# A new list schedule for the first six tiles: two transposes by DMA, weights in smaller pieces, two loads queued earlier

## The chip, the cores and the metric

The kernel runs on one core of one Trainium2 chip. The metric is the device time of one execution in microseconds (us). Each comparison ran both kernels in turn on the same chip. Profiles are of single executions; their span is about 2 us shorter than the execution's time.

## The reference

```python
# x: (8, 1024, 768) float32, w_qkv: (768, 2304) float32, gamma: ones, eps: 1e-5
def reference(x, gamma, w_qkv, eps):
    rms = np.sqrt(np.mean(x ** 2, axis=-1, keepdims=True) + eps)
    x_norm = x / rms * gamma
    return np.matmul(x_norm, w_qkv).astype(np.float32)
```

The 8,192 rows make 64 tiles of 128 rows. K = 768 is six blocks of 128. The result of a tile is 2,304 columns: four products' worth of 512 and one of 256, each summed over the six blocks in PSUM, the buffer that TensorE's results go to.

## The kernel before

TensorE (PE in the profiles) does the products; VectorE (DVE), ScalarE (ACT) and GpSimd (POOL) scale weights and share the casting and copying; SyncE (SP) issues the DMA transfers. A tile needs x transposed (K on the partitions). Tiles 6 to 63 get that by a transposing DMA; tiles 0 to 3, and before the change 4 and 5, by TensorE. The first six tiles, the "head", are computed while the weights arrive, so their order is a hand-made list with planned times. The list only sorts the instructions; at run time each engine takes its own in that order and waits on semaphores. All loads of x and of weights, all stores and all DMA transposes go through SyncE's one queue.

```python
ARRIVALS = "xxxwwwxwwwwwxxwww"     # order of the head's loads: x tiles, weight pieces
PIECES = [... six of (one K block, columns 0:512), (0, 3, 512, 512), (3, 6, 512, 512),
          (0, 6, 1024, 512), (0, 6, 1536, 512), (0, 6, 2048, 256)]   # k0, k1, column, columns
HEAD_PLAN = [ ... (16.47, "cast", 4, "DVE"), ... (17.24, "tr", 4), ... (18.02, "cp", 4, "DVE"), ...]
...
def tr(t):                         # transpose on TensorE, into PSUM; cp copies it out
    for ko in range(KO):
        nc.tensor.transpose(out=PT[t][:, ko, :], in_=XB[t][:, ko * P:(ko + 1) * P], identity=ident)

def trans_dma(t):                  # transpose by DMA, straight to SBUF
    nc.sync.dma_start_transpose(out=XT[t], in_=XB[t])
...
# a store is put one plan-us after the evacuation that completes its 1,024 columns
elif left[t, h] == 0:
    at(time + gap, store, t, h, *PARTS[h])
...
for t in range(HEAD, MT):          # the steady tiles
    at(now - 15, load_x, t)
    at(now - 8.5, cast, t)
    at(now - 7.5, trans_dma, t)
    at(now - 5, stat, t)
    at(now - 3, recip, t)
    for n0 in range(0, N, NT):
        at(now, mm, t, n0, range(KO))
        ...
```

## Time and profile before

| | before |
|---|---|
| time, median of 3 | 389.47 us (389.18 to 389.60) |
| profiled span | 387.9 us |
| TensorE busy | 379.5 us, 98% |
| steady tile | 5.83 us |
| DMA | 308 GB/s on average, 379 to 397 while the head loads and stores |
| waits of TensorE after 15 us | one, 0.4 us, tile 7's transposed x |

The lines themselves stand in the prediction. In the timeline a row is a run of equal instructions on one engine: start, length, engine, line, operation, output and inputs, count, and in brackets the engine's idle time before it with what ended it. The windows view gives, for a stretch of time, each engine's busy time with its instructions in brackets, then the granted TensorE clock, the DMA engines' busy share and their GB/s.

Bookkeeping helps here: a product of 512 columns starts 0.216 us after the one before. A larger distance between starts is a wait, and these distances give TensorE's lost time a little more truly than the idle times in brackets, since busy times are drawn longer (0.38 us) than the pace.

### The profile page before, as it was taken

To read this page: it belongs to the slowest core of one execution; us is meant where nothing else is said; L and a number is where in the kernel's file an instruction comes from. 1 tells how busy PE (TensorE), PEld (TensorE's weight loads), DVE (VectorE), ACT (ScalarE), POOL (GpSimd) and SP (SyncE) were. 2 spreads that over 40 slices of the span, in tenths; PEclk is the share of its full clock that TensorE was granted. 3 is DMA by queue.
4 is the path that set the end of the run, shared out by engine and by line. 5 is a ranking of instruction groups with operands and counts; after the bars stand their busy time and mean duration, and the time that the engine had idled before them with its cause. 6 is when DMAs were issued, how large, how long until landed. Compare 5 with 4: busy or idle time off the path is not lost.

```text
span 387.9 us, 5500 instructions
## 1 busy us (share of the span) xinstructions
PE 379.5 (98%) x1953; PEld 194.3 (50%) x1992; DVE 159.1 (41%) x317; ACT 178.1 (46%) x359; POOL 5.9 (2%) x12
## 2 busy tenths in 40 slices
PE   7999999999999999999999999999999999999996
PEld 6444644554554554554554554554554554554553
DVE  3667634343433343433343433343334343334332
ACT  6652234544444544444534444534434535434532
POOL 1310000000000000000000000000000000000000
PEclk9999999999999999999999999999999999999999
DMA  7999999999999999999999999999999999999974
GB/s 272 392 384 358 308 369 284 397 301 274 333 311 305 279 326 295 290 330 300 276 346 288 302 317 280 318 311 304 287 318 301 297 318 303 287 325 292 292 264 189
DMA packets 87606, 119.51 MB, mean 308 GB/s; under 512 B 50710, under 2 KB 59676, under 8 KB 87580
## 3 DMA queue, kind: packets, MB, share of 16 engines
q1 hardware_dynamic: 87568, 119.17, 100.7%
q8 instruction: 15, 0.25, 0.3%
q14 instruction: 11, 0.09, 0.1%
q10 hardware_dynamic: 12, 0.00, 0.0%
HBM read 32.25 MB, written 75.50 MB: 278 GB/s over the span
## 4 chain that ended last, share of the span: by engine, by line
PE 94%; DMA 3%; SPq 1%; issue 1%; DVE 0%; ACT 0%
PE pm L216 94%; DMA w_f<-in_w_qkv_dram 2%; DMA xT<-xb 2%; SPq L140 0%; SPq L145 0%; PE pm L183 0%; DVE w_b L151 0%; ACT ot L232 0%; DVE ot L230 0%
## 5 line engine op out<-in xcount | busy, mean ns | idle before, releaser
L216 PE MATMUL pm<-w_b,xT 128*128 128x512 bf16 (+1 forms) x1881 | 372.4, 357 | 3.0 <-DMA xT<-xb 0.4
L216 PEld LDWEIGHTS <-xT 128*128 128x128 bf16 x1920 | 187.6, 98 | 186.6 <-issue 0.8
L230 DVE TENSOR_SCALAR ot<-pm,rstd 128x512 f32<-128x512 f32 (+1 forms) x168 | 116.7, 696 | 210.3 <-PE pm L216 210.3
L232 ACT ACTIVATE ot<-pm,rstd 128x512 f32<-128x512 f32 (+1 forms) x152 | 97.9, 645 | 187.0 <-PE pm L216 141.7
L170 ACT ACTIVATE sq<-x_t 128x768 bf16<-128x768 f32 x64 | 53.4, 834 | 10.2 <-DMA x_t<-in_x_dram 10.2
L159 DVE CAST xb<-x_t 128x768 bf16<-128x768 f32 x61 | 33.2, 545 | 4.1 <-DMA x_t<-in_x_dram 4.0
L172 ACT ACTIVATE rms<-ssq,eps_sb 128x1 f32<-128x1 f32 x64 | 18.8, 294 | 2.1
L170 ACT ACTIVATION_READ_ACCUMULATOR sq<-x_t 128x1 f32 x64 | 12.2, 191 | 0.0
L177 DVE RECIPROCAL rstd<-rms 128x1 f32<-128x1 f32 x64 | 9.8, 153 | 0.0
L151 DVE TENSOR_SCALAR w_b<-w_f,g_sb 128x512 bf16<-128x512 f32 (+1 forms) x14 | 6.5, 494 | 6.1 <-DMA w_f<-in_w_qkv_dram 6.0
L153 ACT ACTIVATE w_b<-w_f,g_sb 128x512 bf16<-128x512 f32 (+1 forms) x10 | 6.1, 651 | 5.7 <-DMA w_f<-in_w_qkv_dram 5.7
L155 POOL TENSOR_SCALAR w_b<-w_f,g_sb 128x512 bf16<-128x512 f32 (+1 forms) x6 | 5.2, 864 | 23.5 <-DMA w_f<-in_w_qkv_dram 23.5
L265 PE MATMUL pm<-warm 128*128 128x128 bf16 x35 | 3.8, 300 | 1.0 <-DVE eps_sb L124 1.0
L265 PEld LDWEIGHTS <-warm 128*128 128x128 bf16 x35 | 3.5, 142 | 1.0 <-DVE eps_sb L124 1.0
L197 PE MATMUL pm<-ident_f,x_t 128*128 128x128 f32 x18 | 2.8, 292 | 0.8 <-DMA x_t<-in_x_dram 0.8
L197 PEld LDWEIGHTS pm<-ident_f,x_t 128*128 128x128 f32 x18 | 2.2, 155 | 1.1 <-DMA x_t<-in_x_dram 1.0
L127 ACT ACT_TABLE_LOAD x1 | 1.3, 1283 | 1.3 <-PEq L325 1.3
L159 DVE CAST xT<-pm 128x512 bf16<-128x512 f32 (+1 forms) x3 | 1.7, 596 | 0.0
L159 DVE COPY xT<-pm 128x768 bf16<-128x768 bf16 x3 | 1.6, 547 | 0.0
L248 DVE COPY g_sb<-pm 128x6 f32<-128x6 f32 x1 | 0.2, 165 | 3.6 <-PE pm L247 3.6
L183 PEld LDWEIGHTS <-xb 128*128 128x128 bf16 x18 | 1.2, 98 | 0.9 <-DVE xb L159 0.6
L183 PE MATMUL pm<-ident,xb 128*128 128x128 bf16 x18 | 1.5, 220 | 0.0
(13 smaller groups left out, 3.1 us busy)
## 6 DMA issues: line engine op xcount, KB each, us to landing
out_dram<-ot SPq DMA_DIRECT2D x126, 512.0 KB, 4.0
x_t<-in_x_dram SPq DMA_DIRECT2D x64, 384.0 KB, 4.3
out_dram<-ot SPq DMA_DIRECT2D x64, 128.0 KB, 3.2
w_f<-in_w_qkv_dram SPq DMA_DIRECT2D x2, 1536.0 KB, 13.3
w_f<-in_w_qkv_dram SPq DMA_DIRECT2D x3, 768.0 KB, 8.5
w_f<-in_w_qkv_dram SPq DMA_DIRECT2D x6, 256.0 KB, 5.8
out_dram<-ot SPq DMA_DIRECT2D x4, 256.0 KB, 2.0
xT<-xb SPq DMA_TRANSPOSE x58, 4.4
```

The source lines that it names most:

```text
L151: nc.vector.tensor_scalar(out=o, in0=i, scalar1=g, scalar2=None, op0=mult)
L153: nc.scalar.activation(out=o, in_=i, func=AF.Copy, scale=g, bias=0.0)
L155: nc.gpsimd.tensor_scalar(out=o, in0=i, scalar1=g, scalar2=1.0, op0=mult, op1=mult)
L159: nc.vector.tensor_copy(out=out, in_=in_)
L170: nc.scalar.activation(out=sq, in_=X[t], func=AF.Square, accum_out=ssq)
L172: nc.scalar.activation(out=rms, in_=ssq, func=AF.Sqrt, scale=inv_k, bias=eps_sb)
L177: nc.vector.reciprocal(out=r, in_=RS[t])
L197: nc.tensor.transpose(out=PT[t, h][:, ko - k0, :], in_=X[t][:, ko * P:(ko + 1) * P], identity=ident_f)
L216: nc.tensor.matmul(out=PM[t, n0][:, :nl], lhsT=XT[t][:, ko, :], rhs=w_b[:, ko, n0:n0 + nl], start=(b == 1), stop=(b == KO))
L230: nc.vector.tensor_scalar(out=o, in0=pm[:, :nl], scalar1=RS[t], scalar2=None, op0=mult)
L232: nc.scalar.activation(out=o, in_=pm[:, :nl], func=AF.Copy, scale=RS[t], bias=0.0)
L265: nc.tensor.matmul(out=wps, lhsT=warm, rhs=warm, start=True, stop=True)
```

## The change

The intent is to take 12 transposes off TensorE, to let weights be scaled as soon as a smaller piece has landed, and to have x of tiles 6 and 7 early. The order of the products in the head changes with it: tiles 0 to 3 do three column blocks before tiles 4 and 5 begin.

```diff
-ARRIVALS = "xxxwwwxwwwwwxxwww"
-PIECES = [..., (0, 3, 512, 512), (3, 6, 512, 512), (0, 6, 1024, 512), (0, 6, 1536, 512), (0, 6, 2048, 256)]
+HEAD = 6
+PIECES = [..., (0, 2, 512, 512), (2, 4, 512, 512), (4, 6, 512, 512), (0, 3, 1024, 512), (3, 6,
+          1024, 512), (0, 3, 1536, 512), (3, 6, 1536, 512), (0, 6, 2048, 256)]
+LOADS = [
+    (-9.00, "x", 0), (-8.99, "x", 1), (-8.98, "x", 2), (-8.97, "w", 0), (-8.96, "w", 1),
     ... cut: pieces 2 to 9, x tiles 3 and 4
+    (-8.85, "w", 10), (-8.84, "x", 5), (18.73, "t", 4), (18.74, "w", 11), (22.11, "t", 5),
+    (22.12, "w", 12), (22.13, "w", 13), (22.14, "x", 6), (22.15, "x", 7),
+]
 HEAD_PLAN = [
     ... the whole list is new; "tr" and "cp" of tiles 4 and 5 are gone
 ]
-HEAD_END = 44.51
+HEAD_END = 43.73
@@ the loads of the head
+    for time, kind, n in LOADS:
+        at(time, {"x": load_x, "w": load_w, "t": trans_dma}[kind], n)
@@ the steady tiles
-        at(now - 15, load_x, t)
+        if ("x", t) not in {q[1:] for q in LOADS}:
+            at(now - 15, load_x, t)
```

## The prediction

> **What bounds the kernel now.** I read the page from the top, then zoomed into the first 60 us, the only part that the change touches (six "head" tiles of 128 rows that are computed while the weights are still arriving; tiles 6 to 63 then run one after the other). The summary and the group of matrix products:
> ```profile
> span 387.9 us, 5500 instructions
> PE 379.5 (98%) x1953; PEld 194.3 (50%) x1992; DVE 159.1 (41%) x317; ACT 178.1 (46%) x359; POOL 5.9 (2%) x12
> ...
> PEclk9999999999999999999999999999999999999999
> DMA  7999999999999999999999999999999999999974
> ...
> L216 PE MATMUL pm<-w_b,xT 128*128 128x512 bf16 (+1 forms) x1881 | 372.4, 357 | 3.0 <-DMA xT<-xb 0.4
> ```
> The reader is to see one bound, TensorE, with 3.0 us idle ahead of its products in the whole run. The chain of waits gives their pace: its repeating pieces of 9.46, 9.46 and 10.10 us, with 0.05 between, hold 150 recorded products plus a missing one here and there, five tiles in 29.16 us: 5.83 us a tile, 0.216 us for a product of 512 columns (24 a tile) and half for one of 256 (6). 64 tiles need 64 x 5.83 = 373.2 us. So the change can win only what stands between the products in the head, and whatever it makes TensorE wait is lost for good.
>
> The timeline of TensorE, start to end:
> ```profile
> 8.48 2.10 PE L216 MATMUL pm<-w_b,xT 128*128 128x512 bf16 x8 [0.39 <-POOL w_b L155]
> 10.52 0.51 PE L183 MATMUL pm<-ident,xb 128*128 128x128 bf16 x6
> 11.19 6.80 PE L216 MATMUL pm<-w_b,xT 128*128 128x512 bf16 x30 [0.15 <-DVE w_b L151]
> 17.82 0.50 PE L183 MATMUL pm<-ident,xb 128*128 128x128 bf16 x6
> 18.20 0.81 PE L216 MATMUL pm<-w_b,xT 128*128 128x512 bf16 x2
> 18.85 0.50 PE L183 MATMUL pm<-ident,xb 128*128 128x128 bf16 x6
> 19.18 31.94 PE L216 MATMUL pm<-w_b,xT 128*128 128x512 bf16 x165
> 51.56 0.60 PE L216 MATMUL pm<-w_b,xT 128*128 128x512 bf16 x2 [0.44 <-DMA xT<-xb]
> ```
> Three groups of six transposes stand between products; from 19.18 on nothing stops TensorE until 51.56, where tile 7 waits for its transposed x. At 19.18, 138 of the head's 180 products are left (102 of 512 columns, 36 of 256): 22.0 + 3.9 = 25.9 us, so tile 6 begins at 45.1.
>
> TensorE is not the only full engine: the DMA row is full too, and the third view, the timeline of the DMA queue (start, time to issue), tells how late its work lands:
> ```profile
> 19.83 7.14 SPq L236 DMA_DIRECT2D out_dram<-ot  x6
> 27.27 0.34 SPq L140 DMA_DIRECT2D x_t<-in_x_dram  x1
> ...
> 38.37 1.95 SPq L206 DMA_TRANSPOSE xT<-xb  x1
> ```
> The first store, issued at 19.83, lands 10.8 us later, at 30.7 (the view of the store's line in that window). The load of tile 6, issued at 27.27, is used at 37.78: VectorE and ScalarE start on it only then, both released by that transfer. One queue, in order, about 10 us deep.
>
> **What the Trainium skill says.** "DMA: Bandwidth & Descriptors", section "Queues, rings and completion order": each DMA engine consumes its descriptors in ring order, and all that SyncE issues shares one row of rings. The trace agrees: late-issued small transfers land only after the big ones ahead. "TensorE: Matmul & The Clock Gate", section "Wait — 56ns, not 53.3ns?": warm products start 55.6 ns (128 columns) and 215.7 ns (512) apart; the trace has 0.216 us, and the chain has 0.34 us for six transposes, 57 ns each. Same page, "What's actually happening": after an idle window of some 3.4 us the clock falls to half, and it takes about as long a busy stretch to come back. The trace shows the fall: the last product ends at about 384.4, and the granted clock is 1.00 in 384.4:386.8 and 0.52 in 386.8:387.9.
>
> **The change part by part.**
> 1. Transposes of tiles 4 and 5 leave TensorE: 12 x 57 ns = 0.68 us saved; their two copies out of PSUM leave VectorE, which has room.
> 2. First weights: piece 0 is now scaled on VectorE (0.49 us against GpSimd's 0.69), piece 1 on GpSimd. All the same the fifth weight piece lands when it did (the bytes ahead of it are the same, 11.3 us), and by its scaling at 11.8 TensorE has done 12 products and 6 transposes in both kernels. So 0 gained.
> 3. Weights of columns 512 to 1535 in halves and thirds, so that scaling starts on smaller pieces: removes the wait of about 0.13 us near 14.5 (two starts 0.345 apart instead of 0.216). TensorE's order becomes tiles 0 to 3 on three column blocks, then tiles 4 and 5. With no wait, from the 24th product on (14.44), tile 4 begins after 48 more, 14.44 + 10.37 = 24.8; tile 5 at 28.7; tile 6 after 15.55 more, at 44.25. That is 0.85 ahead of 45.1, and agrees with the 0.78 by which the schedule's own end moves.
> 4. Loads of tiles 6 and 7 go earlier, so tile 7's wait, about 0.6 us of TensorE time by its start-to-start gap, should go. Best case: 0.85 + 0.6 = 1.45 us faster.
> 5. The two transposes by DMA, and here I see the loss. The built program shows the queue's order: loads, transpose of tile 4, piece 11 (768 KB), four stores of 512 KB, **then** the transpose of tile 5, then pieces 12 and 13, tiles 6 and 7. Ahead of tile 5's transpose stand six x tiles (2,304 KB), 12 weight pieces (5,376 KB) and four stores (2,048 KB): 9,728 KB. In the old kernel its first store was the end of just that many, 9,216 + 512 = 9,728 KB, and landed at 30.7. Add the two transposes' own time on the DMA engines. Those of 38.37 and 45.48 took 6.1 and 6.0 us to land, and around the first of them the DMA moved 79 GB/s in 42:44 against 393 in 8.4:18. From the landings I take 0.6 to 2 us each. Tile 5's xT lands at 31.9 to 34.7, say 33.3.
> 6. Tile 4's transpose is issued after its cast, at about 19.7 to 20.7, and with 6 us to landing is there at 25.7 to 26.7, against a need at 24.8: 1 to 2 us of wait, but it only shifts time: tile 5 would then be wanted at about 29.7 and wait some 3.6.
> The sum: tile 5 begins at 33.3 instead of 28.7, so tile 6 at 33.3 + 15.55 = 48.85, and tile 7 at 54.7 against 51.56: +3.1 us. A wait of over 3 us may also drop the clock for a while: half speed for up to 3.4 us costs up to 1.7 us, at perhaps one chance in three to one half: +0.5. Later waits look safe: pieces 12 and 13 land near 35.5 and 37.5 and are wanted at 41 and 45; tile 6's xT is there before 46.
>
> **The rivals.** (a) The schedule holds as written: 1.45 us faster, 388.0. For it: it was presumably planned with known arrival times. Against it: it scales piece 12 only 3 us after piece 11, which leaves room for one piece (2 us) and a transpose, not for 2 MB of stores (4.9 us at the 1.22 us per 512 KB I read between landings), though the queue has them between. (b) The stores overtake nothing but the transposes stall the DMA queue more, 2 us and over each, and tile 7 or 8 waits again behind the stores of columns 1024 to 2047, which now come in a burst (each tile's 512 KB every 0.65 us instead of every 1.3): 394 to 396. (c) DMA slack swallows it: the DMA engines run slightly ahead or transposes cost little (0.6 us each), so tile 5 waits 2 us only: about 390.5. A bound by VectorE or ScalarE I don't see: 41 and 46% busy.
>
> **Range and chances.** 389.47 + 3.1 + 0.5 - 0.4 (I give (a) and (c) some weight) = 392.7. From 389.6, (c) with a small wait, to 395.2, (b). 2% is 7.8 us: a gain of that is impossible, since the products alone need 373 of a span of 387.9 and the other 15 are start and drain that the change keeps; a loss of that needs several rivals at once. Faster 0.01, same 0.95, slower 0.04.
>
> **What will show it.** In TensorE's timeline: 6 L183-type transposes instead of 18; a wait for xT of 0.5 to 2 us near 25, and a longer one, 2.5 to 4.5 us, ending near 33, with a DMA transpose as releaser and the first store's landing well before it; tile 7 without a wait, or under 0.5. In the DMA queue's timeline the second transpose issued behind four stores, its landing 6 us or more after issue. In the clock row, perhaps a slice under 9 near 33. I am wrong if xT of tile 5 is there by 29 (stores that don't hold it back), or if the stall of the DMA at a transpose is far over 2 us.

## The result

The changed kernel took 397.91 us (median of 4, 397.73 to 398.67) against 389.54 for the kernel before: ratio 1.0219, 95% interval 1.0201 to 1.0237. It is slower by over 2%. (A ratio is the mean time of one kernel's runs over that of the other's in the same rounds, so it is not quite the ratio of the medians quoted. Executions over 1.5% slower than the fastest of the same kernel are left out of the means.) On another chip, later, the same file was 396.57 and 396.38 us with ratios of 1.0163 and 1.0153: under 2% there, and 6.3 to 8.4 us slower in all three comparisons.

From the page of the changed kernel, the summary, the clock row and the group of products:

```profile
span 395.6 us, 5525 instructions
PE 384.1 (97%) x1980; PEld 194.2 (49%) x1980; DVE 156.3 (40%) x312; ACT 177.6 (45%) x357; POOL 8.1 (2%) x17
...
PEclk9996999999999999999999999999999999999999
...
L229 PE MATMUL pm<-w_b,xT 128*128 128x512 bf16 (+1 forms) x1920 | 377.1, 359 | 6.1 <-DMA xT<-xb 5.3
```

Idle time before the products rose from 3.0 to 6.1 us, 5.3 of it for xT. Busy time rose too, by 4.6 us, with 12 transposes fewer, and the clock row has a 6 in its fourth slice. (The group counts 1920 products against 1881 before because the old trace lacks some records; each leaves a hole of 0.05 us in the chain, so 39 of them explain about 2 us of the busy time.) So there are waits, and products that ran slowly. TensorE's timeline of the changed kernel:

```profile
11.78 0.51 PE L196 MATMUL pm<-ident,xb 128*128 128x128 bf16 x6
12.38 16.99 PE L229 MATMUL pm<-w_b,xT 128*128 128x512 bf16 x78
33.77 24.23 PE L229 MATMUL pm<-w_b,xT 128*128 128x512 bf16 x120 [4.40 <-DMA xT<-xb]
58.91 16.41 PE L229 MATMUL pm<-w_b,xT 128*128 128x512 bf16 x81 [0.91 <-DMA xT<-xb]
```

Tile 5 waited 4.4 us, and tile 7, at 58.91, waited longer than it did before. The DMA queue's timeline (start, time to issue) and the chain of waits around it:

```profile
20.29 1.32 SPq L219 DMA_TRANSPOSE xT<-xb  x1
21.67 0.57 SPq L158 DMA_DIRECT2D w_f<-in_w_qkv_dram  x1
22.34 2.71 SPq L249 DMA_DIRECT2D out_dram<-ot  x4
25.14 1.73 SPq L219 DMA_TRANSPOSE xT<-xb  x1
```
```profile
25.14 8.58 DMA xT<-xb
33.72 0.05 issue
```

Tile 5's transpose was issued at 25.14 behind four stores and landed 8.58 us later, at 33.72. The store ahead of it landed at 32.9 in the trace. Now the windows view: DMA around the first transpose, and the clock after the long wait.

```profile
18.00:20.50 2.50, 2.50 (x13) 1.16 (x12) 1.81 (x4) 1.74 (x3) 0.98 (x1) 1.00 1.04 383
20.50:22.50 2.00, 2.00 (x11) 0.88 (x9) 1.53 (x5) 1.36 (x4) 0.00 (x0) 1.00 0.73 174
22.50:25.00 2.50, 2.50 (x13) 1.18 (x12) 1.79 (x5) 2.01 (x5) 0.00 (x0) 1.00 0.66 85
25.00:31.50 6.50, 4.37 (x21) 1.76 (x18) 3.40 (x5) 1.29 (x2) 0.98 (x1) 1.00 1.03 395
...
32.40:39.10 6.70, 5.33 (x13) 1.94 (x14) 0.75 (x1) 0.91 (x2) 2.92 (x5) 0.50 1.06 350
```

The last two columns show the DMA dropping from 383 GB/s to 174 and 85 for 4.5 us; the third from the end shows the clock at half in 32.4:39.1. From 33.77 to 39.1 products start 0.427 us apart, about 12 of them, 12.4 x 0.211 = 2.6 us more than at full clock.

In order of time the loss in this execution, measured between starts of tiles: tile 6 would have begun at 33.77 + 15.55 = 49.3 at full clock, against 45.1 before: 4.2 us. The halved clock adds 2.6. Tile 7 waits 1.07 us against 0.61 before (distance to its start, less the pace): 0.5. A wait of 0.23 at tile 10. Together 7.5 of the 7.7 us by which the span grew. This is an account of where time went, not yet of what causes it: the experiments show that these terms do not add freely.

### The profile page after: what moved, and what is told of

Its sections match the earlier page's. It is cut to its first block, busy times and chain, and to the rows that moved or that the text cites. A ratio compares the mean times of both kernels' runs of the same rounds, so it can differ in the third digit from the quotient of the medians.

```text
span 395.6 us, 5525 instructions
## 1 busy us (share of the span) xinstructions
PE 384.1 (97%) x1980; PEld 194.2 (49%) x1980; DVE 156.3 (40%) x312; ACT 177.6 (45%) x357; POOL 8.1 (2%) x17
## 4 chain that ended last, share of the span: by engine, by line
PE 91%; DMA 7%; SPq 1%; issue 0%; DVE 0%; ACT 0%
PE pm L229 91%; DMA xT<-xb 5%; DMA w_f<-in_w_qkv_dram 2%; SPq L158 0%; SPq L153 0%; DVE w_b L164 0%; ACT ot L245 0%
## 5 line engine op out<-in xcount | busy, mean ns | idle before, releaser
L229 PE MATMUL pm<-w_b,xT 128*128 128x512 bf16 (+1 forms) x1920 | 377.1, 359 | 6.1 <-DMA xT<-xb 5.3
L243 DVE TENSOR_SCALAR ot<-pm,rstd 128x512 f32<-128x512 f32 (+1 forms) x166 | 115.1, 695 | 220.9 <-PE pm L229 220.8
L245 ACT ACTIVATE ot<-pm,rstd 128x512 f32<-128x512 f32 (+1 forms) x154 | 99.5, 647 | 193.0 <-PE pm L229 145.4
L166 ACT ACTIVATE w_b<-w_f,g_sb 128x512 bf16<-128x512 f32 (+1 forms) x6 | 3.8, 648 | 14.1 <-DMA w_f<-in_w_qkv_dram 14.1
L168 POOL TENSOR_SCALAR w_b<-w_f,g_sb 128x512 bf16<-128x512 f32 (+1 forms) x11 | 7.4, 686 | 30.9 <-DMA w_f<-in_w_qkv_dram 23.2
L174 ACT CAST xT<-pm 128x256 bf16<-128x256 f32 (+1 forms) x3 | 1.2, 438 | 1.2 <-PE pm L210 1.2
L172 DVE COPY xT<-pm 128x768 bf16<-128x768 bf16 x1 | 0.6, 558 | 0.0
L196 PEld LDWEIGHTS <-xb 128*128 128x128 bf16 x6 | 0.3, 98 | 0.4 <-DVE xb L172 0.4
```

The source lines that it names most:

```text
L166: nc.scalar.activation(out=o, in_=i, func=AF.Copy, scale=g, bias=0.0)
L168: nc.gpsimd.tensor_scalar(out=o, in0=i, scalar1=g, scalar2=1.0, op0=mult, op1=mult)
L172: nc.vector.tensor_copy(out=out, in_=in_)
L229: nc.tensor.matmul(out=PM[t, n0][:, :nl], lhsT=XT[t][:, ko, :], rhs=w_b[:, ko, n0:n0 + nl], start=(b == 1), stop=(b == KO))
L243: nc.vector.tensor_scalar(out=o, in0=pm[:, :nl], scalar1=RS[t], scalar2=None, op0=mult)
L245: nc.scalar.activation(out=o, in_=pm[:, :nl], func=AF.Copy, scale=RS[t], bias=0.0)
```

## The experiments

Sixteen runs, each a variant of the changed kernel unless said otherwise. The question was first whether tile 5's transpose waits for the stores, then where the rest comes from when that wait is taken away. All results were correct.

### t5_first: the four stores behind tile 5's transpose

```diff
-            at(time + gap, store, t, h, *PARTS[h])
+            at(22.115 if (t, h) in {(1, 0), (2, 0), (3, 0), (0, 0)} else time + gap, store, t, h, *PARTS[h])
```

> Only the queue's order is changed: the four stores of 512 KB go behind the transpose of tile 5 instead of ahead of it. Theory A (in-order queue, the transpose of tile 5 waits for 2 MB of stores): its landing moves from 33.7 us to about 29, TensorE's 4.4 us wait falls below 1.5 us, the clock stays at full, and the time falls by 4.5 to 7 us from 397.9, to 391 to 393.5. Rival B (the first transpose stalls the DMA engines and that alone makes the second one late, wherever the stores stand): landing stays at 32 or later, wait of 3 us or more, time above 396.

Measured: 395.19 us (394.05 to 397.77), ratio 1.0114. The landing moved to 27.1 us, and no wait was left at tile 5: theory A holds and B does not, for this wait. But the time is above what A expected. TensorE's timeline of this run (its profiled execution was the slowest of five):

```profile
46.70 6.01 PE L229 MATMUL pm<-w_b,xT 128*128 128x512 bf16 x29 [0.62 <-DMA xT<-xb]
56.74 33.48 PE L229 MATMUL pm<-w_b,xT 128*128 128x512 bf16 x154 [4.04 <-DMA xT<-xb]
```

The wait has moved to tiles 6 and 7. It was long enough again for the clock to halve. What held tile 7's transpose up isn't shown: it was issued at 49.67, 3 us after tile 6 had begun, and took 7.03 us to land.

### t5_mid: two stores ahead, two behind

```diff
-            at(time + gap, store, t, h, *PARTS[h])
+            at(22.115 if (t, h) in {(2, 0), (3, 0)} else time + gap, store, t, h, *PARTS[h])
```

> A dose: two of the four stores go behind the transpose of tile 5. Theory A: its landing moves by two stores, 2 x 1.23 = 2.5 us, to about 31.3, the wait falls from 4.4 to about 2 us. Whether the clock still halves after so short a wait is open: if it does, about 394.5, if not about 392.5. Rival B: nothing moves by over 0.7 us.

Measured: 392.60 us, ratio 1.0071. The landing was 31.1 us, as theory A has it (31.3). Tile 5 waited 1.4 us, the clock stayed at full, and tile 7 waited 1.85 us. So the time is the one expected without a halved clock, by a different split of the waits (a third one, 0.8 us for weight piece 10 at 23.1, lies ahead of everything that this variant moves). Why two stores ahead do better than none (t5_first) isn't settled; in t5_first the two transposes follow each other closely and pieces 12 and 13 land 0.7 and 1.6 us later.

### warm: dummies in the wait

```diff
     for time, op, *args in HEAD_PLAN:
+        if op == "mm" and args[:2] == [5, 0]:
+            at(time - 0.01, idle, 60)
```

> 60 dummy products of 128 columns (60 x 56 ns = 3.3 us) are put into TensorE's wait ahead of tile 5; everything else as in the changed kernel. Theory C: 2.6 us of the loss is the clock halved from 32.3 to 39.1 us after the wait. Then the clock stays at full, the products after 33.8 start 0.216 us apart, tile 5 still begins at about 33.8, and the time falls by about 2.6 us less what tile 7 then waits longer, to 395 to 396. Rival: the clock is a symptom and is paid back later by waits for transfers: tile 7's wait grows from 0.9 to over 2.5 us and the time stays within 0.7 of 397.9.

Measured: 395.60 us, ratio 1.0151. In the profile the clock was at full throughout, and the time fell into the expected range. But tile 7 waited 0.9 us and tile 8 1.8 us, where the changed kernel had no wait at tile 8; and on the changed kernel's second chip its own ratio was 1.0163. Whether the clock cost anything in the end was open; see the square below.

### t5_pe: tile 5 back on TensorE

```diff
-    ..., (18.73, "t", 4), (18.74, "w", 11), (22.11, "t", 5),
+    ..., (18.73, "t", 4), (18.74, "w", 11),
-    (24.42, "evac", 3, 1024, "DVE"), (25.56, "mm", 4, 512, "012345"),
+    (24.42, "evac", 3, 1024, "DVE"), (25.50, "tr", 5), (25.55, "cp", 5, "DVE"), (25.56, "mm", 4, 512, "012345"),
```

> Tile 5 alone is transposed on TensorE again (6 transposes, 0.34 us), tile 4 stays with the DMA. Theory A: no wait for xT of tile 5, no clock drop; 4.6 + 2.6 - 0.34 = 6.9 us of the loss goes, leaving tile 7's wait: 390.5 to 391.5. Rival B': without the second transpose the DMA's stall after the first one still makes a wait for weight pieces 11 to 13 near 30 to 34 us, of over 2 us: above 393.

Measured: 392.92 us, ratio 1.0074: more than expected under A. No wait at tile 5, no halved clock, but tile 7 waited 2.7 us for its xT, which landed at 53.7 us. Rival B' is not it either: no wait for pieces 11 to 13. So three ways of shortening or taking away tile 5's wait (t5_first, t5_mid, t5_pe) each left or made one at tile 7.

### both_pe: tiles 4 and 5 back on TensorE

The diff of t5_pe, and for tile 4:

```diff
-    ..., (18.73, "t", 4), (18.74, "w", 11),
+    ..., (18.74, "w", 11),
-    (21.67, "mm", 0, 1024, "35"), (22.09, "cast", 5, "DVE"), ...
+    (21.62, "tr", 4), (21.65, "cp", 4, "DVE"), (21.67, "mm", 0, 1024, "35"), (22.09, "cast", 5, "DVE"), ...
```

> The changed kernel with tiles 4 and 5 both transposed on TensorE again; weights in thirds and halves, order of work and early loads stay. In t5_pe tile 5's wait was gone, but tile 7 waited 2.7 us for its xT, at 392.9. Theory D: the in-order DMA queue is the second bound of the head, and the transposes of tiles 4 and 5 take DMA time (a stall around each) that tile 7's transpose, at the end of the same 18.9 MB, pays. Then the fourth store lands near 30.5 instead of 33.1, tile 7's xT near 51.5 instead of 53.7, its wait is below 1.3 us, time 389.5 to 390.8. Rival E: the new order (stores of columns 1024 to 2047 in a burst) or the early loads delay tile 7 whoever transposes: wait of 2 us or more, time 391.8 or more.

Measured: 392.06 us (390.68 to 392.65), ratio 1.0046. In the profiled execution (390.68 us) the fourth store landed at 29.9, tile 7's xT at 51.75, and it waited 0.5 us, all as theory D expects and not the 2 us or more of rival E. But this was the fastest of four executions. The median is above D's range of times and inside E's, and which wait the slower three had, no profile shows, so D is shown for one execution only. The windows view of both_pe, for the two stretches in which the changed kernel's DMA fell off:

```profile
20.50:22.50 2.00, 2.00 (x14) 1.01 (x13) 0.65 (x3) 0.90 (x3) 0.00 (x0) 1.00 1.04 391
22.50:25.00 2.50, 2.35 (x15) 1.12 (x13) 2.49 (x7) 1.81 (x4) 0.00 (x0) 1.00 1.04 415
```

391 and 415 GB/s against 174 and 85: (391 - 174) x 2.0 + (415 - 85) x 2.5 = 1,260 KB not moved, some 3 us of the queue at its full rate. That is what tile 4's transpose cost the queue, though tile 4 itself never waited.

### t4_after_w11: starvation or stall?

The diff of t5_pe, and weight piece 11 queued ahead of tile 4's transpose:

```diff
-    ..., (18.73, "t", 4), (18.74, "w", 11),
+    ..., (18.74, "w", 11), (18.75, "t", 4),
```

> As t5_pe, with weight piece 11 queued ahead of tile 4's transpose, so that the queue has work while it waits for tile 4's cast. In t5_pe the queue moved little between 20.5 and 25 us. Theory G (starvation: SyncE stands at the transpose until the cast is done): piece 11 lands near 25 instead of 28, the fourth store near 31 instead of 33.1, tile 7's wait falls from 2.7 to about 1 us; tile 4's xT lands near 26, later than its 25.3, for up to 1 us of wait: 391 to 392. Theory H (the stall follows the transpose wherever it stands): the fourth store still lands at 32.5 or later, tile 7's wait stays over 2 us, time 392.5 or more.

Measured: 392.12 us, ratio 1.0057 (t5_pe 1.0074, on another chip; the intervals overlap). Its windows view:

```profile
20.50:22.50 2.00, 2.00 (x11) 0.92 (x10) 1.11 (x3) 1.31 (x4) 0.00 (x0) 1.00 1.03 387
22.50:25.00 2.50, 2.47 (x12) 1.03 (x11) 2.03 (x6) 1.80 (x4) 0.00 (x0) 1.00 1.37 161
```

The first stretch is whole again, the second is not. So there are two costs. One is starvation: SyncE takes its instructions in order and stands at the transpose until tile 4's cast is done (20.3 us in the changed kernel), with nothing queued behind. The other stays with the transpose: around it the DMA engines move 161 GB/s instead of 415, (415 - 161) x 2.5 = 635 KB, about half of the 1,260. Their mean share of 1.37 hides two phases, as steps of half a microsecond of the same run show:

```profile
22.50:23.00 0.50, 0.47 (x3) 0.16 (x2) 0.50 (x3) 0.08 (x1) 0.00 (x0) 1.00 1.78 330
23.00:23.50 0.50, 0.50 (x3) 0.19 (x2) 0.50 (x2) 0.50 (x1) 0.00 (x0) 1.00 3.32 169
23.50:24.00 0.50, 0.50 (x4) 0.24 (x3) 0.24 (x1) 0.47 (x3) 0.00 (x0) 1.00 0.73 55
24.00:24.50 0.50, 0.50 (x4) 0.24 (x3) 0.29 (x2) 0.50 (x2) 0.00 (x0) 1.00 0.21 41
24.50:25.00 0.50, 0.50 (x4) 0.19 (x2) 0.50 (x1) 0.26 (x1) 0.00 (x0) 1.00 0.82 209
```

First the share is high; then, for about 1 us, little moves (55 and 41 GB/s, the share down to 0.21), although SyncE had begun to issue the stores at 21.67. Most of the 635 KB, some 470, are lost after 23.5. Why the engines stand there, no run shows. Piece 11 landed at 25.0 instead of 28.0, the fourth store at 31.3 instead of 33.1, tile 7's xT at 52.0 instead of 53.7; tile 8 waited 0.6 us instead. Theory G has the larger part in the landings; in the time, which both theories' ranges nearly meet at, the gain is not shown.

### x67_back and x67_rep: early loads of tiles 6 and 7 undone

```diff
-    (22.12, "w", 12), (22.13, "w", 13), (22.14, "x", 6), (22.15, "x", 7),
+    (22.12, "w", 12), (22.13, "w", 13),
```

> The changed kernel with only the early loads of tiles 6 and 7 undone (they go back among the stores). Theory D: they move the same bytes through the same queue ahead of tile 7's transpose, so nothing of the loss goes: tile 5 waits 4.4 us and the clock halves as before, tile 7 waits 0.9 to 2 us, 397.3 to 399. Rival F: the early loads push the stores back and cause tile 7's wait: it goes, and the time falls by 1 us or more, to 396.9 or less.

Measured: 396.20 us, ratio 1.0155, which looked like a gain over 1.0219. The profile spoke against it: tile 5's wait was 1 us shorter, and those loads stand behind its transpose. So both kernels ran again side by side.

> The changed kernel once more, on the chip of the next three. Theory: 397 to 398.7 as before; TensorE waits some 4.4 us for tile 5's xT and the clock is halved for about 6.8 us. If it waits only 3.4 us here, with the clock halved for one stretch of 3.4 us, and comes out near 396, the gap to x67_back was the chip's or the run's, not the loads'.

> The same file as x67_back, beside the changed kernel this time. Theory D: within 0.8 us of the changed kernel on this chip, since the early loads stand behind tile 5's transpose and cannot reach its wait. Rival F: 1 us or more faster than the changed kernel, with a shorter wait at tile 7.

Measured: the changed kernel 396.57 us (395.26 to 398.38), ratio 1.0163; x67_rep 397.01 (394.25 to 397.73), ratio 1.0160. No difference. The gap of x67_back was between chips or runs. In the profile of after_rep the wait at tile 5 was 3.1 us and the clock halved for one stretch of 3.4 us instead of 6.8, so the same file varies by as much.

### both_pe_lead and before_lead: tiles 7 to 9 transposed earlier

```diff
     for t in range(HEAD, MT):
+        lead = {7: 3.0, 8: 2.0, 9: 1.0}.get(t, 0.0)
-            at(now - 15, load_x, t)
-        at(now - 8.5, cast, t)
-        at(now - 7.5, trans_dma, t)
+            at(now - 15 - lead, load_x, t)
+        at(now - 8.5 - lead, cast, t)
+        at(now - 7.5 - lead, trans_dma, t)
```

> As both_pe, and cast and DMA transpose of tile 7 come 3 us earlier in the list, of tile 8 2 us, of tile 9 1 us, with the loads of 8 and 9. Theory D: tile 7's transpose passes four stores of 512 KB in the queue and lands before 47, no wait at tile 7, and none at 8 or 9 over 0.5 us: 388.3 to 389.5, level with the kernel before or up to 1 us better. Rival: the delay moves on to tiles 8 to 10, whose transposes queue behind the displaced stores: sum of waits unchanged from both_pe.

Measured: 390.46 us, ratio 1.0019 (both_pe 1.0046 beside it). From 27 us to the end the waits view has one row of 0.2 us. So with both transposes back and tile 7 ahead of the stores the loss is all but gone (1.0001 to 1.0038; both_pe's 1.0024 to 1.0069 overlaps it). But it is not the 388.3 to 389.5 expected: without a wait the new order of work is still not faster than the old, and why is open.

> The kernel before, with cast and transpose of tile 7 3 us earlier in the list, of tile 8 2 us, of tile 9 1 us, and the loads of 7 to 9 earlier by the same. Its one wait past 20 us, 0.6 us at tile 7, should go and nothing take its place: 0.4 to 0.7 us faster than the kernel before. Rival: the displaced stores make a later tile wait, no gain or a loss.

Measured, on the kernel before: 389.46 us (389.27 to 390.95) against 390.08, ratio 0.9987, interval 0.9968 to 1.0007. After 12 us the waits view of TensorE is empty. The gain expected (0.4 to 0.7 us) is there in the medians, but is not clear of noise.

### dma_fixed: both DMA transposes kept, their places mended

The diffs of t5_first and of both_pe_lead, with piece 11 ahead of tile 4's transpose.

> The changed kernel with both DMA transposes kept and their places in the queue mended: piece 11, then tile 4's and tile 5's transposes, then the four stores; and tiles 7 to 9 cast and transposed earlier, as in both_pe_lead. Theory: no wait over 1 us and no clock drop; the 12 TensorE transposes (0.68 us) are saved, tile 4 waits up to 1 us for its xT near 25.7: 389.5 to 391, level with the kernel before. Rival: the DMA time of the two transposes still comes out somewhere (pieces 12 and 13, or tile 6), with a wait of 2 us or more: 392 or more.

Measured: 393.02 us, ratio 1.0062, in the rival's range. No halved clock, but in its profile, the slowest of six executions, 1.2 us of wait for weight piece 10's scaling at 24.5, 1.2 us for xT at 59.8 and another of that size at 72.9. The rival had a wait of 2 us or more at pieces 12 and 13 or at tile 6; none is there. And the wait for piece 10 can't be a cost of the transposes, since piece 10 stands ahead of both in the queue; other profiles have between nothing and 0.9 us at this point. So the time says that a cost remains, and the profile does not say whose.

### The square: clock and queue

A halved clock slows TensorE, and that may give the queue time to catch up, so that the clock's loss and a later wait overlap. So four corners on one chip: changed kernel, dummies, earlier transposes of tiles 7 to 9, both.

> The changed kernel, first corner of the square: 396 to 398.5.

> Dummies in tile 5's wait alone. If the clock's loss is real and stays saved: 1.5 to 2.6 us below after_rep2. If it comes back at tiles 7 and 8 because the DMA queue is the bound there: within 0.8 us of after_rep2, with waits at tiles 7 and 8 together 1.5 us or more longer.

> Earlier casts and transposes of tiles 7 to 9 alone, with the clock still halved after tile 5's wait: tile 7's wait of about 1 us goes, 0.7 to 1.3 us below after_rep2.

> Both. If the payback at tiles 7 and 8 is only their place in the queue, the two savings add: 2.5 to 4 us below after_rep2, with tile 5's wait the one loss left, 393 to 394.5. If the DMA queue has no slack to give, waits at tiles 7 to 10 stay at 2 us or more and the time is within 2 us of after_rep2.

| | as changed | tiles 7 to 9 earlier |
|---|---|---|
| clock may halve | 396.38 us, 1.0153 (1.0125 to 1.0181) | 396.56 us, 1.0166 (1.0141 to 1.0192) |
| dummies in the wait | 395.97 us, 1.0161 (1.0133 to 1.0189) | 394.39 us, 1.0104 (1.0082 to 1.0127) |

Neither measure alone gains anything; both together gain 0.5%, 2 us (the intervals of the two corners just touch). So of the expectations, lead's gain of 0.7 to 1.3 us did not come, and warm_lead's 2.0 us falls short of "the two add" (2.5 to 4) and stands at the edge of "no slack" (within 2). One of warm_rep's six executions (398.71) had a mean clock of 0.991, so the dummies did not always hold it. TensorE's timeline of warm_rep, whose profile has the clock at 0.998:

```profile
29.35 3.51 PE L278 MATMUL pm<-warm 128*128 128x128 bf16 x60
33.15 21.59 PE L229 MATMUL pm<-w_b,xT 128*128 128x512 bf16 x117 [0.29 <-DMA xT<-xb]
55.58 6.01 PE L229 MATMUL pm<-w_b,xT 128*128 128x512 bf16 x30 [0.83 <-DMA xT<-xb]
62.58 27.61 PE L229 MATMUL pm<-w_b,xT 128*128 128x512 bf16 x136 [1.00 <-DMA xT<-xb]
```

and of lead:

```profile
33.23 4.88 PE L229 MATMUL pm<-w_b,xT 128*128 128x512 bf16 x11 [4.04 <-DMA xT<-xb]
38.32 36.69 PE L229 MATMUL pm<-w_b,xT 128*128 128x512 bf16 x195 [0.22 <-issue]
76.94 13.35 PE L229 MATMUL pm<-w_b,xT 128*128 128x512 bf16 x66 [1.93 <-DMA xT<-xb]
```

In warm_rep tiles 7 and 8 wait instead (0.8 and 1.0 us, against 0.7 and 0.5 in after_rep2's profile, so not the 1.5 us more that was expected of a payback); in lead, where tile 7 doesn't wait, tile 10 does, by 1.9 us at 76.9. In warm_lead the waits for xT in the profile are 0.9 us at tile 5 and 1.2 at 62.7, and its best and worst executions were 393.17 and 395.50.

So time won in one place is partly lost at a later transpose. That is not because the queue's bytes pile up until then. The changed kernel's windows from 42 us on:

```profile
42.00:44.00 2.00, 2.00 (x11) 0.91 (x10) 0.00 (x0) 0.00 (x0) 0.00 (x0) 1.00 0.50 100
44.00:46.00 2.00, 2.00 (x11) 0.94 (x10) 0.75 (x1) 0.32 (x1) 0.00 (x0) 1.00 0.00 0
```

In the second stretch the DMA engines stand empty: SyncE waited 2.8 us, until 45.85, at a store for VectorE's result, and VectorE for TensorE's products. All that SyncE had issued had landed by then, so no bytes were owed from 20.5:25. SyncE's order, in which transposes stand behind stores that wait for TensorE, is the likelier link; no run tests it alone.

## Why the prediction was wrong

It said slower, by about 3.2 us and within 2%; measured were 8.4 us and 2.2%. The wait of tile 5 behind the stores was right; two other steps failed, tile 7's wait and the clock. In the profiled execution the loss by tile 6 was 4.2 us (3.75 expected), the clock took 2.6 (0.5) and tile 7's longer wait 0.5 (a gain of 0.6 expected).

- **Part 5, tile 5 behind the stores: right.** Landing expected at 33.3, measured 33.72. t5_mid moved it by two stores' time (to 31.1), t5_first to 27.1. The count of KB ahead was a good ruler. (The line under the chain of waits misreads it: three pieces of 49 are 147 recorded products, and 150 with the missing ones. The five tiles in 29.16 us are right.)
- **Part 1, 12 transposes off TensorE: right, and unimportant.** Six remain in the timeline.
- **Part 2, the first weights: 0 gained.** Here the fifth piece's first product began at 12.38, 0.5 us later than in the old kernel (11.84). In the profiles of the variants that same point, with nothing changed ahead of it, lies anywhere between 11.4 and 12.8, once at 13.3 (after_rep2), so I take no effect of the change from it.
- **Part 6, tile 4: wrong, harmlessly.** I took 6 us to landing from two transposes that stood in a full queue; this one, the last in the queue, landed 3.1 us after its issue, at 23.35, and tile 4 didn't wait. The 6 us were the queue's, not the transpose's; tile 6's, issued at 41.75 into an emptied queue, took 2.7.
- **The clock term: mis-sized.** I gave 0.5 us to a halved clock (at most 1.7, with a chance of one third to one half). In that profile it took 2.6 us, over two stretches of 3.4 us. "TensorE: Matmul & The Clock Gate" ("What's actually happening") gives an idle window of some 3.4 us; the trace of before had shown the fall 2.4 us after the last product. A wait that I expected to be near 4 us should have had a high chance of it.
- **Part 4 and "tile 7 without a wait": the step that failed.** Part 4 took tile 7's wait of 0.6 us to be for its x, and so to go with the earlier load. Tile 7 waited 1.07 us, more than before. The old trace shows what it waits for:

```profile
45.33 0.15 DVE ot L230
45.48 6.04 DMA xT<-xb
```

Its x had landed at 41.2 (issued at 36.12, 5.1 us to landing). Its transpose was issued at 45.48 only, behind the head's last stores, and took 6.04 us. I estimate tile 6's begin as tile 7's start less its wait and 5.83 us; then tile 7's transpose was issued 0.4 us after it in the old kernel, 1.2 in the changed one, 1.1 in both_pe and 2.5 in t5_pe, with 5.3 to 6.1 us to landing. That leaves a wait each time. The runs agree: undoing the early loads changes nothing (x67_rep), and the transposes of tiles 7 to 9 moved forward take tile 7's wait away (both_pe_lead, where it was issued at 42.10, before_lead, lead). The rest of "Later waits look safe" held: pieces 12 and 13 were there near 35.7 and 38.1, and tile 6 did not wait.
- **The sum.** I summed the loss on TensorE alone, one wait plus what follows, and looked at the DMA queue only for the landing of tile 5's transpose. But when tile 5's wait or the clock's loss was taken away, tiles 6 to 10 waited more. What holds the later transposes up in each variant was not taken apart. The part of the change that costs is the pair of DMA transposes: with both undone the ratio is 1.0046, against 1.0155 for x67_back, which keeps them, on the same chip.
- **The range.** Its upper end, 395.2, came from rival (b), "the transposes stall the DMA queue more, and tile 7 or 8 waits again", without the clock. Rival (b) with the halved clock comes nearest to what happened. Of its stalls of 2 us and over, the first transpose had one (some 3 us, SyncE's wait included), the second did not (0.8 us from the store ahead of it to its landing).

The remaining loss of both_pe, 0.46%, is not settled beyond this: with tile 7 moved forward it was 0.19%, and the two intervals overlap. How the DMA engines lose time around a DMA transpose was not taken apart, beyond that about half of it was SyncE's wait for the cast and most of the rest a standstill after the first phase.

## What to carry to other kernels

When two resources are nearly full, price a change on both: here 0.7 us saved on TensorE was paid with about 3 us on the DMA queue for one transpose alone, and a mended wait came up again three tiles on (lead). In an in-order queue count the KB ahead of a transfer to know when it lands, and never queue one whose source isn't ready ahead of others that are. Before you move a load earlier, look up whether the wait ends with that load or with a later step, here a transpose queued behind stores. A wait of TensorE that nears 3 us should be valued with the clock it may lose, but test that loss in place: it can overlap with another resource's delay and then cost nothing by itself.

## What the Trainium skill lacked or had wrong

- "Advanced Engine Details and Errata", section "X-Bar Transpose (TRN2)", says that transposing DMAs are as fast as regular ones. Here one of 192 KB cost the queue more than a transfer of its size would: in the 2.5 us around it the engines moved 161 GB/s (t4_after_w11), with stores issued behind it, against 415 without it (both_pe), 635 KB less.
- "DMA: Bandwidth & Descriptors", section "Queues, rings and completion order", describes ring order, and no page gives the cost of an issuing engine that waits, in order, for a transfer's source: 174 GB/s in 20.5:22.5 against 391 without the transpose there.
- No page I found gives the time from issue to landing of a DMA transpose: 3.1 us at the queue's end (changed kernel, tile 4), 8.6 us behind four stores (tile 5).
- "TensorE: Matmul & The Clock Gate" gives a window of about 3.4 us, and the runs agree. It does not say how busy a window must be to count as idle, nor whether one or two of them follow a wait. Here waits of 3.3 to 4.6 us (distance of starts, less the pace) were each followed by one or two stretches of 3.4 us at half clock, and waits up to 2.8 us (t5_pe) between products by none. But in after_rep2 the clock also halved for one stretch at 7.5:10.9, after a wait of 1.7 us in a stretch (4.1:7.4) in which TensorE was busy for 1.67 of 3.30 us. In dma_fixed as long a wait (1.65 us, ending at 7.91) was followed by none.
